# A residual block at its turn to gate_up: ScalarE's copies and halves of h2 in order, and the first y behind the third set's sums

## The chip, the cores and the metric

The kernel runs on one core of one Trainium2 chip. The metric is the device time of one execution in microseconds. Three executions before the change took 1344.05 us in the median (1343.78 to 1344.97).

## What is computed

One block of a hybrid encoder, for 1024 rows of 1024 numbers, all in float32:

```python
h = rmsnorm(x, norm_mix_pre)
m = mixer(h, ...)                 # gated short convolution + forgetting attention, merged, times w_out
x = x + rmsnorm(m, norm_mix_post)
h = rmsnorm(x, norm_ffn_pre)      # called h2 here
g, u = split(h @ w_gate_up)       # w_gate_up: 1024 x 5632, g and u 1024 x 2816
f = (silu(g) * u) @ w_down        # silu(g) = g * sigmoid(g)
x = x + rmsnorm(f, norm_ffn_post)
```

The change lies between the second `rmsnorm` and the first columns of `silu(g) * u`.

## The kernel before

Every float32 product is made of three matmuls of a rounded half and a rest: `split(hi, lo, src)` writes `hi` on ScalarE (a copy) and `lo = src - hi` on VectorE, and `mm3` multiplies hi·hi, hi·lo and lo·hi. The large products use a Strassen scheme with seven block products. For gate_up, the moving side is h2 in seven forms: B11, B21, B22 and the sums T1 to T4, each with a hi and a lo half. The stationary side is a pair of weight blocks for one column f of 128 (gate and up): A11, A12, A22 and the sums S1 to S4.

The tiles that matter here:

- `um`: h2, transposed, 8 x 128 x 1024. `e_norm(st)` (L1248) makes one slice of 128 rows: two sums of squares, a scale, the addition of x, a second scale into `tt`, the store of `xt` to `x2_dram`, eight TensorE transposes into `tp` and two ScalarE copies from `tp` into `um`. The eighth slice, st = 7, is the last.
- `hah`, `hal`: the halves of B11 and B21, from the first four slices.
- `hth`, `htl` and `hch`, `hcl`: the halves of T1 to T4 and of B22. `h2_sums(sl)` (L1317) makes them for one slice of each half of the rows, sl = 0 to 3, and needs slices sl and 4 + sl of `um`: on VectorE two sums into `sx` and two into tiles `c22`, on ScalarE the four hi halves, on VectorE the four lo halves.
- `raw` (3 buffers), `hi` (4), `lo` (3), `sx` (1), `s4` (1): the weights of a column as loaded, their halves and their sums.
- `c12`, `c21`, `c22` (2 buffers each): results of a column. In the profile they all appear as `c`, the PSUM banks as `b`.
- `z`: two buffers that xt, c11 (a column's first result, g1 below) and `sgf` (the sigmoid) take in turn.

The order of the stage as written: columns 0 to 6 (NPRE = 7) get their first two products early, since these need only B11 and B21. `f_first(f)` (L1282) makes A11·B11, copies it out (p1), goes on in the same bank with A12·B21, copies that out (c11, the first quarter of g) and stores both to `pre_dram`. `f_first(0)` to `f_first(3)` stand ahead of `e_norm(7)`, `f_first(4)` to `f_first(6)` between the four `h2_sums`. Then the loop over all 22 columns (L1361):

```python
for f in range(NF):
    if f < NPRE:
        p1 = t_(fp, "c21")
        nc.gpsimd.dma_start(p1, pre_dram[f][0])
        g1 = z_tile("c11", w=NC)
        nc.gpsimd.dma_start(g1, pre_dram[f][1])
        _, g2, u1_, u2 = strassen(rest.get(), hb, psm, fp, p1)
```

`strassen` (L505) makes the five products left, of 12 matmuls each, in the order S2·T2, S1·T1, S3·T3, S4·B22, A22·T4. Behind each stands a VectorE addition of the bank to a result; the first, `add(c12, p1, b2)`, reads p1 and has to be done before S3·T3 goes on in the same bank. c21 is the tile of p1. `rest.get()` keeps the operands of two columns ready: on its first call it prepares sets 0 and 1, on its second, in column 1, the third one, set 2. A set (`prep_rest`, L444) is two loads into `raw` and

```python
sub(s3, a11, a21)
add(s1, a21, a22)
sub(s2, s1, a11)
split(hx, lx, sx)      # S2 and S3
split(h2, l2, r2)      # S1 and A22
sub(s4, a12, s2)
split(h4, l4, s4)      # S4
```

After `strassen`, a column's y is made in `um` (free by then), half by half: a ScalarE sigmoid into `sgf`, `sgf * g` and `sgf * u` on VectorE. Every second column, `y_sums` makes sums of two y for the product with w_down and stores them to `a_dram` from GpSimd's queue.

What sets the order: Python only traces the instructions. A planner then writes out each engine's queue from its own reckoning of when operands and buffers are ready, so an instruction whose inputs are early may stand well ahead of its place in the source. At run time each engine works through its queue strictly in that order. Where `strict[0]` names an engine, each of its instructions is pinned behind the one traced last on that engine (L76: `keep_in_program_order`); the pin is an order, not a wait for the other to finish. In the stage of the change `strict[0]` was empty. All instructions pass through one helper, so the profile gives L74 as the line of all; tiles tell them apart.

Of the kernel before, what the change touches and what calls it, by code (L numbers as in the profile page):

```python
# [12 lines left out]
AF = mybir.ActivationFunctionType  # L13
# [8 lines left out]
ST = S // P  # L22
# [23 lines left out]
def block_kernel(  # L46
# [17 lines left out]
    strict = [()]  # L64

    class InOrder:
# [15 lines left out]
    nc = SimpleNamespace(  # L82
        **{e: InOrder(e) for e in engines}
    )
# [7 lines left out]
    def pool(name, bufs=1, side="left", space=None):  # L92
        kw = dict(name=name, bufs=bufs)
        if space is not DRAM:
            kw["reuse_waits"] = "tile"
        if space is not None:
            kw["space"] = space
        else:
            kw["side"] = side
        stack = ExitStack()  # L100
        ctx.callback(stack.close)
        return stack.enter_context(tc.tile_pool(**kw)), stack.close
# [4 lines left out]
    def add(o, a, b):  # L107
        nc.vector.tensor_tensor(o, a, b, op=ALU.add)
# [4 lines left out]
    def mul(o, a, b):  # L113
        nc.vector.tensor_tensor(o, a, b, op=ALU.mult)

    def copy(o, a):
        nc.scalar.activation(o, a, AF.Copy)
# [14 lines left out]
    cpool, _ = pool("const")  # L132
    stat, _ = pool("stat", 4, side="right")
    dpool, _ = pool("dram", space=DRAM)
# [40 lines left out]
    def st_tile(name, w=1):  # L175
        return stat.tile([P, w], F32, tag=name, name=name)
# [24 lines left out]
    def z_tile(name, dt=F32, w=S):  # L201
        return zp.tile([P, S], dt, tag="z", name=name, bufs=2)[:, :w]
# [146 lines left out]
    for st in range(ST):  # L349
        ops, rest = cur  # L350
# [19 lines left out]
    wpool, _ = pool("w")  # L370
# [107 lines left out]
    def bank(psp, name):  # L478
        return psp.tile([P, NC], F32, tag="mm", name=name)

    def prod(ps, w, b, first):
        (ah, al), (bh, bl) = w, b
        kw = {} if first else dict(skip_group_check=True)
        for k in range(4):
            mm3(
                ps,
                (ah[:, k, :], al[:, k, :]),
                (bh[:, k, :], bl[:, k, :]),
                first and k == 0,
                k == 3,  # L490
                **kw,
            )

    def t_(tmp, name):
        return tmp.tile([P, NC], F32, tag=name, name=name)
# [9 lines left out]
    def strassen(w, hb, psp, tmp, p1=None):  # L505

        b1 = None
        if p1 is None:
            b1 = bank(psp, "b1")
            prod(b1, w["A11"], hb[B11], True)  # L510
            p1 = t_(tmp, "c21")
            copy(p1, b1)
        b2, b3 = bank(psp, "b2"), bank(psp, "b3")
        prod(b2, w["S2"], hb[T2], True)
        c12 = t_(tmp, "c12")
        add(c12, p1, b2)
        prod(b3, w["S1"], hb[T1], True)
        c22 = t_(tmp, "c22")
        add(c22, p1, b3)
        if b1 is not None:  # L520
            prod(b1, w["A12"], hb[B21], False)
        prod(b2, w["S3"], hb[T3], False)
        add(c22, c22, b2)
        prod(b3, w["S4"], hb[B22], False)
        add(c12, c12, b3)
        prod(b2, w["A22"], hb[T4], False)
        c21 = p1
        add(c21, p1, b2)
        return b1, c12, c21, c22
# [21 lines left out]
    psm, psm_close = pool("psm", 6, space=PSUM)  # L551
    n1, n2 = slice(0, NC), slice(NC, S)

    def wcols(c0):
        return win[:, c0 : c0 + P]
# [270 lines left out]
    for ij, (kind, j, _, _) in enumerate(jobs):  # L826
# [4 lines left out]
        if ij < 2:  # L831
            if ij == 0:
# [7 lines left out]
                for n, (w, _) in enumerate(heads):  # L840
                    b1, b2 = bank(psm, "b1"), bank(psm, "b2")
                    p1, c11 = t_(pp, "c21"), t_(pp, "so")
# [14 lines left out]
            w = {**w, **(prep_rest(wcols(jobs[ij][3]), r1) if ij else rest0)}  # L857
            if ij == 1:
                pairs.q.append(pairs.prep(*pairs.srcs.popleft()))
            _, c12, c21, c22 = strassen(w, h1b, psm, pp, p1)  # L860
# [7 lines left out]
        else:  # L868
            w = pairs.get()
# [63 lines left out]
    def sg_tile():  # L933
        return tp_.tile([P, NC], F32, tag="sg", name="sg", bufs=4)
# [24 lines left out]
    was, sgs = {}, {}  # L959
# [203 lines left out]
    psm, psm_close = pool("psm2", 8, space=PSUM)  # L1163
# [30 lines left out]
    for n in range(2):  # L1194
        ns = slice(n * NC, (n + 1) * NC)
        for d in range(KT):
            ds_ = slice(d * P, (d + 1) * P)
            sg = sg_tile()
# [23 lines left out]
    fp, fp_close = pool("f", 2)  # L1222
# [20 lines left out]
    def load_xt(st):  # L1243
        xt = z_tile("xt")
        nc.sync.dma_start(xt, x2d[st * P : (st + 1) * P, :])
        return xt

    def e_norm(st, pm):  # L1248
        ss = slice(st * P, (st + 1) * P)
        xt = xts.popleft()  # L1250
        if st + 1 < ST:
            xts.append(load_xt(st + 1))
        tt = ep.tile([P, D], F32, tag="t", name="tt", bufs=1)
        s2 = st_tile("s2", 2)
        for n in range(2):
            ns = slice(n * NC, (n + 1) * NC)
            nc.scalar.activation(tt[:, ns], pm[n], AF.Square, accum_out=s2[:, n : n + 1])
        ssq = st_tile("ssq")
        add(ssq, s2[:, 0:1], s2[:, 1:2])
        rs = rms_scale(ssq)  # L1260
        for n in range(2):
            ns = slice(n * NC, (n + 1) * NC)
            nc.vector.scalar_tensor_tensor(
                tt[:, ns], pm[n], rs, gpo[:, ns], op0=ALU.mult, op1=ALU.mult
            )
        add(xt, xt, tt)
        nc.gpsimd.dma_start(x2_dram[ss, :], xt)
        ssq = st_tile("ssq")
        nc.scalar.activation(tt, xt, AF.Square, accum_out=ssq)
        rs = rms_scale(ssq)  # L1270
        nc.vector.scalar_tensor_tensor(tt, xt, rs, gpr, op0=ALU.mult, op1=ALU.mult)
        for q in range(2):
            tp = psm.tile([P, 4, P], F32, tag="mm", name="tp")
            for k in range(4):
                kt = 4 * q + k
                nc.tensor.transpose(tp[:, k, :], tt[:, kt * P : (kt + 1) * P], ident)
            copy(um[:, 4 * q : 4 * q + 4, ss], tp)

    def f_src(f):
        return wgu[:, f * P : (f + 1) * P], wgu[:, FH + f * P : FH + (f + 1) * P]  # L1280

    def f_first(f):  # L1282
        w, _ = prep_first(f_src(f)[0])
        b1, p1 = strassen_first(w, hb, psm, fp)
        c11 = t_(fp, "c12")
        copy(c11, b1)
        nc.gpsimd.dma_start(pre_dram[f][0], p1)
        nc.gpsimd.dma_start(pre_dram[f][1], c11)

    hb = [(hah[:, q], hal[:, q]) for q in range(2)]  # L1290
# [26 lines left out]
    def h2_sums(sl):  # L1317
        a = slice(sl * P, (sl + 1) * P)
        b = slice(NC + sl * P, NC + (sl + 1) * P)
        b11, b12 = um[:, 0:4, a], um[:, 0:4, b]  # L1320
        b21, b22 = um[:, 4:8, a], um[:, 4:8, b]
        u = wtile("sx", 1).rearrange("p (t k) s -> p t k s", t=2)
        sub(u[:, 0], b12, b11)
        sub(u[:, 1], b22, u[:, 0])
        split(hth[:, 0:2, :, a], htl[:, 0:2, :, a], u)
        for n, x in enumerate(((b22, b12), (b21, u[:, 1]))):
            w = t_(fp, "c22").rearrange("p (k s) -> p k s", k=4)
            sub(w, *x)
            split(hth[:, 2 + n, :, a], htl[:, 2 + n, :, a], w)
        split(hch[:, :, a], hcl[:, :, a], b22)  # L1330

    for sl in range(4):
        if 4 + sl < NPRE:
            f_first(4 + sl)
        h2_sums(sl)


    wd = wdn.rearrange("(k h p) d -> h p k d", h=2, p=P)
# [4 lines left out]
    def y_slot(f):  # L1343
        return um[:, 4 * (f // 2 % 2) + f % 2, :]
# [13 lines left out]

    rest = Pairs([f_src(f) for f in range(NPRE)], prep_rest_alone)
    whole = Pairs([f_src(f) for f in range(NPRE, NF)])  # L1360
    for f in range(NF):  # L1361
        if f < NPRE:
            p1 = t_(fp, "c21")
            nc.gpsimd.dma_start(p1, pre_dram[f][0])
            g1 = z_tile("c11", w=NC)
            nc.gpsimd.dma_start(g1, pre_dram[f][1])
            _, g2, u1_, u2 = strassen(rest.get(), hb, psm, fp, p1)
        else:
            g1, g2, u1_, u2 = strassen(whole.get(), hb, psm, fp)
        if f == NPRE - 1:  # L1370
            whole.q.append(whole.prep(*whole.srcs.popleft()))
        yf = y_slot(f)
        sgs = z_tile("sgf")
        for g, u, ns in ((g1, u1_, n1), (g2, u2, n2)):
            sg = sgs[:, ns]
            nc.scalar.activation(sg, g, AF.Sigmoid)
            mul(sg, sg, g)
            mul(yf[:, ns], sg, u)
        if f % 2:
            y_sums(f // 2)  # L1380
        if f == NF - 2:
            ra, rb = pairs_of(raw_t()), pairs_of(raw_t())
            nc.sync.dma_start(ra, a_dram["A11"][0].rearrange("k p c -> p k c"))
            nc.sync.dma_start(rb, wd[0][:, 0:2, n1])
            down0 = [(pairs_of(hi_t()), pairs_of(lo_t())) for _ in range(2)]
            split(*down0[0], ra)
            split(*down0[1], rb)
# [140 lines left out]
    p1, c22, c11, c12 = (quarter(s_) for s_ in (4, 6, 0, 2))  # L1528
# [109 lines left out]
```

## Time and profile before

| | |
|---|---|
| median of three runs | 1344.05 us (1343.78 to 1344.97) |
| the profiled execution's own time | 1344.87 us |
| its span, first to last instruction | 1343.1 us |
| granted TensorE clock, mean | 0.998 |
| stage of `f_first` and the h2 halves | from 701.5 us to 742.2 us |
| columns 0 to 6 | from 742.2 us to about 841 us |

The profile is one execution. PE is TensorE, DVE VectorE, ACT ScalarE, POOL GpSimd, SP the queue of most loads. A row of a timeline has the start, the duration, the engine, the operation, and output <- inputs by tile name; the bracket at its end says how long the engine had been idle before and what ended it. Matmuls overlap, so their starts, not their durations, tell the pace.

### The profile page before, as it was taken

The page shows a single profiled execution, that of the slowest core. Times are in us where ns is not written, and L with a number is a line of the kernel's source. Part 1 is how long each engine was busy: PE and PEld are TensorE (multiplying, and loading weights), DVE is VectorE, ACT ScalarE, POOL GpSimd, SP SyncE. Part 2 cuts the span into 40 slices and gives each one's busy share as a digit, 9 for nine tenths or more (in the row PEclk, how much of TensorE's full clock was granted, in tenths as well). Part 3 has the DMA queues.
Part 4 walks back from the last instruction along what each step waited for, and adds up shares of the span by engine and source line. Part 5 has one row for each costly group of instructions (what it writes and reads, how often), then busy time and mean ns, then how long its engine had stood idle before and what let it go on. Part 6 is the DMA issues. An engine that isn't in the chain of part 4 may idle for free. (4 is left out here: it accounts for less than half of the span.)

```text
span 1343.1 us, 17663 instructions
## 1 busy us (share of the span) xinstructions
PE 1320.6 (98%) x6725; PEld 1096.9 (82%) x6725; DVE 935.2 (70%) x1451; ACT 533.7 (40%) x851; POOL 127.2 (9%) x252
## 2 busy tenths in 40 slices
PE   7999999999999999999999999999999999999997
PEld 7988888888887878788887888888888888888886
DVE  6883767755546767775668898777677766677585
ACT  6641322243345756514446322223222323444452
POOL 0001000011112212000002121110011001000000
PEclk9999999999999999999999999999999999999999
DMA  7242422333325445362235554332333336966541
GB/s 221 91 122 87 136 61 79 119 123 97 108 89 173 158 142 189 105 218 79 94 124 174 185 186 155 103 116 71 112 106 114 101 104 244 366 233 197 157 165 63
DMA packets 153397, 186.86 MB, mean 139 GB/s; under 512 B 9424, under 2 KB 106768, under 8 KB 153312
## 3 DMA queue, kind: packets, MB, share of 16 engines
q1 hardware_dynamic: 138576, 137.19, 32.7%
q0 software_dynamic: 14736, 48.54, 9.5%
q8 instruction: 52, 0.85, 0.3%
q14 instruction: 33, 0.27, 0.1%
HBM read 136.62 MB, written 49.09 MB: 138 GB/s over the span
## 5 line engine op out<-in xcount | busy, mean ns | idle before, releaser
L74 DVE TENSOR_TENSOR c<-c,b 128x512 f32<-128x512 f32 x195 | 133.2, 683 | 85.5 <-PE b L74 67.1
L74 DVE TENSOR_TENSOR lo<-raw,hi 128x1024 fp32r<-128x1024 f32 (+1 forms) x93 | 112.1, 1205 | 82.5 <-PE b L74 70.5
L74 ACT ACTIVATE hi<-raw 128x1024 fp32r<-128x1024 f32 (+1 forms) x100 | 101.7, 1018 | 124.6 <-PE b L74 77.5
L74 PE MATMUL b<-hth,lo 128*128 128x512 f32 x352 | 137.1, 390 | 0.2 <-DVE lo L74 0.2
L74 PE MATMUL b<-hth,hi 128*128 128x512 f32 x352 | 137.1, 390 | 0.0
L74 ACT ACTIVATE hi<-sx 128x1024 fp32r<-128x1024 f32 x41 | 43.6, 1063 | 235.3 <-PE b L74 207.6
L74 PE MATMUL b<-htl,hi 128*128 128x512 f32 x352 | 137.0, 389 | 0.0
L74 PEld LDWEIGHTS b<-hth,lo 128*128 128x128 f32 x352 | 66.1, 188 | 14.3 <-DVE lo L74 0.6
L74 PEld LDWEIGHTS b<-hth,hi 128*128 128x128 f32 x352 | 66.1, 188 | 14.0 <-DVE c L74 0.3
L74 PEld LDWEIGHTS b<-htl,hi 128*128 128x128 f32 x352 | 66.1, 188 | 13.6
L74 DVE TENSOR_TENSOR lo<-sx,hi 128x1024 fp32r<-128x1024 f32 x41 | 50.2, 1224 | 31.1 <-PE b L74 29.4
L74 PE MATMUL b<-hah,hi 128*128 128x512 f32 x176 | 69.2, 396 | 1.8 <-ACT c L74 1.8
L74 PE MATMUL b<-hal,hi 128*128 128x512 f32 x176 | 69.3, 394 | 0.0
L74 PE MATMUL b<-hah,lo 128*128 128x512 f32 x176 | 69.0, 393 | 0.0
L74 DVE TENSOR_TENSOR sx<-raw 128x512 f32<-128x512 f32 x78 | 53.7, 688 | 20.6 <-DMA raw<-in_w_in_dram 10.6
L74 PE MATMUL pd<-hi,lo 128*128 128x512 f32 x160 | 62.3, 389 | 0.0
L74 PE MATMUL pd<-hi 128*128 128x512 f32 x160 | 62.0, 390 | 0.0
L74 PE MATMUL pd<-ghi 128*128 128x512 f32 x148 | 57.7, 390 | 0.0
L74 PE MATMUL pd<-glo,ghi 128*128 128x512 f32 x148 | 57.6, 389 | 0.0
L74 PE MATMUL pd<-ghi,glo 128*128 128x512 f32 x148 | 57.6, 389 | 0.0
L74 PE MATMUL b<-hT34h,hi 128*128 128x512 f32 x136 | 53.1, 390 | 0.4 <-DVE c L74 0.4
L74 PE MATMUL b<-hT12h,lo 128*128 128x512 f32 x136 | 52.9, 389 | 0.0
(362 smaller groups left out, 3361.7 us busy)
## 6 DMA issues: line engine op xcount, KB each, us to landing
raw<-in_w_gate_up_dram SPq DMA_DIRECT2D x51, 512.0 KB, 3.8
raw<-in_w_in_dram SPq DMA_DIRECT2D x35, 512.0 KB, 3.9
a_dramS<-um POOLq DMA_DIRECT2D x44, 256.0 KB, 2.8
a_dramA<-um POOLq DMA_DIRECT2D x33, 256.0 KB, 2.7
xt<-in_x_dram SPq DMA_DIRECT2D x16, 512.0 KB, 4.6
sg<-sg_dram SPq DMA_DIRECT2D x32, 256.0 KB, 4.3
graw<-a_dramS SPq DMA_DIRECT2D x14, 512.0 KB, 4.1
sg_dram<-c POOLq DMA_DIRECT2D x24, 256.0 KB, 2.3
```

The source lines that it names most:

```text
L74: ins = getattr(self.engine, name)(*args, **kw)
```

## The change

Three orders are pinned, and the first y is made later in the source. Nothing is computed otherwise.

- In `e_norm`, for st = 7, the two copies of `tp` into `um` are pinned on ScalarE.
- In `h2_sums(3)`, the four hi halves are pinned on ScalarE: each behind the one before, the first behind the last half of `h2_sums(2)`.
- The sigmoids and products of a column's y move into a function `silu_up`. For column 0 it is called in column 1, behind `rest.get()`, and both that call of `rest.get()` (set 2) and `silu_up(0)` are pinned on VectorE and ScalarE. The instruction traced ahead of set 2's first sum is column 0's last VectorE addition, `add(c21, p1, b2)`. For columns 0 to 6 `rest.get()` now stands ahead of the two loads from `pre_dram`.

```diff
+            if st == ST - 1:
+                strict[0] = ("scalar",)
             copy(um[:, 4 * q : 4 * q + 4, ss], tp)
+            strict[0] = ()
...
     for sl in range(4):
         if 4 + sl < NPRE:
             f_first(4 + sl)
+        if sl == 3:
+            strict[0] = ("scalar",)
         h2_sums(sl)
+    strict[0] = ()
...
+    def silu_up(f, blocks):
+
+        yf = y_slot(f)
+        sgs = z_tile("sgf")
+        for g, u, ns in blocks:
+            sg = sgs[:, ns]
+            nc.scalar.activation(sg, g, AF.Sigmoid)
+            mul(sg, sg, g)
+            mul(yf[:, ns], sg, u)
+
     for f in range(NF):
         if f < NPRE:
+            if f == 1:
+                strict[0] = ("vector", "scalar")
+            w = rest.get()
+            if f == 1:
+                silu_up(0, y0)
+                strict[0] = ()
             p1 = t_(fp, "c21")
             nc.gpsimd.dma_start(p1, pre_dram[f][0])
             g1 = z_tile("c11", w=NC)
             nc.gpsimd.dma_start(g1, pre_dram[f][1])
-            _, g2, u1_, u2 = strassen(rest.get(), hb, psm, fp, p1)
+            _, g2, u1_, u2 = strassen(w, hb, psm, fp, p1)
         else:
             g1, g2, u1_, u2 = strassen(whole.get(), hb, psm, fp)
         if f == NPRE - 1:
             whole.q.append(whole.prep(*whole.srcs.popleft()))
-        yf = y_slot(f)
-        sgs = z_tile("sgf")
-        for g, u, ns in ((g1, u1_, n1), (g2, u2, n2)):
-            sg = sgs[:, ns]
-            nc.scalar.activation(sg, g, AF.Sigmoid)
-            mul(sg, sg, g)
-            mul(yf[:, ns], sg, u)
+        blocks = ((g1, u1_, n1), (g2, u2, n2))
+        if f == 0:
+            y0 = blocks
+        else:
+            silu_up(f, blocks)
         if f % 2:
             y_sums(f // 2)
```

## The prediction

> **What bounds the kernel now.** I read the page's totals first, then TensorE's waits over the whole span, then the stage in which the one avoidable wait lies.
>
> ```profile
> span 1343.1 us, 17663 instructions
> PE 1320.6 (98%) x6725; PEld 1096.9 (82%) x6725; DVE 935.2 (70%) x1451; ACT 533.7 (40%) x851; POOL 127.2 (9%) x252
> ...
> PE tp L74 <- DVE hn L74: 7.8, 1, 7.8
> PE b L74 <- ACT c L74: 1.8, 1, 1.8
> ```
>
> TensorE is busy for 98% of the span, so an edit can only gain where TensorE stands still or runs slowly. Its longest wait is the start, 7.8 us. The next is one wait of 1.8 us for a ScalarE copy (ACT c), and it lies where the h2 halves are made. The windows around it (columns: window, its length, busy time and count of PE, PEld, DVE, ACT, POOL, granted clock, DMA share, GB/s) and the timelines of TensorE and ScalarE (start, duration, what; in brackets the idle time before and what ended it):
>
> ```profile
> 723.00:726.00 3.00, 1.17 (x6) 0.65 (x5) 0.69 (x1) 2.99 (x5) 0.31 (x1) 1.00 0.79 245
> 726.00:729.00 3.00, 3.00 (x10) 2.32 (x9) 1.90 (x3) 2.76 (x5) 0.77 (x2) 0.56 0.63 199
> ```
>
> ```profile
> 721.10 1.03 PE L74 MATMUL tp<-ident,tt 128*128 128x128 f32 x8
> ...
> 723.12 0.39 PE L74 MATMUL b<-hah,lo 128*128 128x512 f32 x1
> 725.34 0.50 PE L74 MATMUL b<-hah,hi 128*128 128x512 f32 x1 [1.83 <-ACT c L74]
> ...
> 726.81 0.63 PE L74 MATMUL b<-hah,lo 128*128 128x512 f32 x1
> 727.24 0.63 PE L74 MATMUL b<-hah,hi 128*128 128x512 f32 x1
> ...
> 729.79 0.40 PE L74 MATMUL b<-hah,hi 128*128 128x512 f32 x1
> ...
> 767.34 0.39 PE L74 MATMUL b<-hch,s4h 128*128 128x512 f32 x1
> ...
> 780.94 0.39 PE L74 MATMUL b<-hch,s4h 128*128 128x512 f32 x1
> ```
>
> ```profile
> 720.22 0.58 ACT L74 ACTIVATE c<-b 128x512 f32<-128x512 f32 x1
> 722.88 1.28 ACT L74 ACT_TABLE_LOAD   x1 [2.08 <-DMA x_dram<-xt]
> 724.17 0.63 ACT L74 ACTIVATE sgf<-c 128x512 f32<-128x512 f32 x1
> 724.71 0.58 ACT L74 ACTIVATE c<-b 128x512 f32<-128x512 f32 x1
> 725.18 1.08 ACT L74 ACTIVATE um<-tp 128x512 f32<-128x512 f32 x2
> ```
>
> The last view holds the story. At 720.80 ScalarE reaches the sigmoid of y 0, which the planner had floated up to this place. Its output tile sgf is one of two z buffers, and the store of xt has to leave it first: 2.08 us, then 1.28 us of table load, then the sigmoid. Queued behind it are the copy c, for which TensorE waits, and the copies of the last transposes into um, whose eight transposes began at 721.10. The copy starts at 724.71 and TensorE goes on at 725.34. Around 727 its matmuls start 0.43 us apart (726.81, 727.24), nearly twice the usual, and the granted clock of that stretch is 0.56.
>
> **The change, part by part.** *The early sigmoid goes (a gain).* y 0 is now traced behind the third set's sums, pinned there on ScalarE and VectorE, so no sigmoid can stand at 720.80. The copy c follows at once. From 723.12 to 729.79 there are 13 matmul starts in 6.67 us; at 0.227 us each (from column 1's fourth product at 767.34 to column 2's at 780.94 are 60 starts in 13.60 us) they take 2.95 us. The loss is **3.72 us**, 2.0 us of it standing still and 1.7 us at half rate. What is late next, if ScalarE is free? Nothing in this place: ScalarE stood idle there until the sigmoid's buffer was free.
>
> The Trainium skill, "TensorE: Matmul & The Clock Gate", section "Why this matters for your kernels", says that only a gap above about 3 us between bursts sends the clock back to half. The trace shows half rate after 1.83 us of idle time. By that rule the half-rate spell would have another cause than this gap and could stay (a rival below).
>
> *The halves of h2 (a small gain).* The pins hold the last slice's four halves on ScalarE in the order of the source. They can't start before um is copied, 725.18 before, about 722 after.
>
> ```profile
> 724.83 0.69 DVE L74 TENSOR_TENSOR sgf<-sgf,c 128x512 f32<-128x512 f32 x1 [1.85 <-ACT sgf L74]
> ...
> 741.72 1.23 DVE L74 TENSOR_TENSOR lo<-sx,hi 128x1024 fp32r<-128x1024 f32 x1 [0.40 <-ACT hi L74]
> ...
> 742.42 0.39 PE L74 MATMUL b<-htl,hi 128*128 128x512 f32 x1
> 743.00 0.50 PE L74 MATMUL b<-hth,lo 128*128 128x512 f32 x1 [0.18 <-DVE lo L74]
> ```
>
> Column 0's first product waits a little for set 0's low half: 743.00 less 742.42 less 0.23, or **0.35 us**. TensorE will arrive there 3.7 us earlier. VectorE's chain to that half starts with um, which comes about 3 us earlier, it stands still less between (1.85 us for the sigmoid), and it no longer makes the first product of y 0. I take the 0.35 us as gained; the bounds are that gain and a loss of 0.7 us (3.7 less 3).
>
> *The third set's sums and y 0 move back (a cost).* Set 2's first sum is now pinned on VectorE behind column 0's last addition, its halves follow in order, and y 0's sigmoids and products follow those. Times here are on the clock of before; all of it moves with TensorE.
>
> ```profile
> 752.39 0.69 DVE L74 TENSOR_TENSOR sx<-raw 128x512 f32<-128x512 f32 x1 [0.67 <-DMA raw<-in_w_gate_up_dram]
> ...
> 756.19 0.68 DVE L74 TENSOR_TENSOR s<-raw,sx 128x512 f32<-128x512 f32 x1
> ...
> 758.26 0.69 DVE L74 TENSOR_TENSOR sgf<-sgf,c 128x512 f32<-128x512 f32 x1
> 758.98 0.69 DVE L74 TENSOR_TENSOR um<-sgf,c 128x512 f32<-128x512 f32 x1
> 759.60 0.68 DVE L74 TENSOR_TENSOR c<-c,b 128x512 f32<-128x512 f32 x1
> ...
> 761.33 0.68 DVE L74 TENSOR_TENSOR um<-sgf,c 128x512 f32<-128x512 f32 x1
> ...
> 767.54 1.23 DVE L74 TENSOR_TENSOR lo<-raw,hi 128x1024 fp32r<-128x1024 f32 x1 [0.59 <-PE b L74]
> 768.68 0.68 DVE L74 TENSOR_TENSOR c<-c,b 128x512 f32<-128x512 f32 x1
> ```
>
> ```profile
> 756.99 0.63 ACT L74 ACTIVATE s4h<-s 128x512 fp32r<-128x512 f32 x1 [1.27 <-DVE s L74]
> 757.52 0.62 ACT L74 ACTIVATE sgf<-c 128x512 f32<-128x512 f32 x1
> ```
>
> The first sum goes from 752.39 to 760.28, behind the addition of 759.60. Set 2's second low half waited for a buffer until column 1's third product ended, 767.54, and still does. But S4's difference, 756.19 before, is traced behind it and is now pinned there: 768.68 to 769.37. Its high half follows 0.12 us later (756.87 to 756.99), at 769.49; the table load comes 0.53 us behind it (756.99 to 757.52), at 770.02; the sigmoid at 771.31 (722.88 to 724.17). The two products follow 0.66 and 0.72 us on (724.17 to VectorE's product at 724.83; 758.26 to 758.98), so the first half of y 0 is done at 773.38, where it was done at 762.01.
>
> Who waits for that? The buffer of c21, which that product reads, takes p1 of column 2, and column 2's first addition needs p1 ahead of its third product:
>
> ```profile
> 762.42 0.56 POOL L74 DMA_DIRECT2D a_dramA<-um  x1 [12.30 <-DVE um L74]
> 762.97 0.54 POOL L74 DMA_DIRECT2D c<-pre_dram  x1
> ...
> raw<-in_w_gate_up_dram SPq DMA_DIRECT2D x8, 512.0 KB, 4.3
> c<-pre_dram POOLq DMA_DIRECT2D x6, 256.0 KB, 3.4
> ```
>
> Behind the product come 0.41 us to GpSimd's store (762.01 to 762.42), 0.55 us to the load, 3.4 us to its landing: 777.74. The addition takes 0.68 us and hands over at about 778.5. TensorE wants that bank for its third product, 12 matmuls ahead of the fourth at 780.94, at 778.22. So the two meet, and I price a **stall of 0.3 us**; the ends are none (the load 0.3 us quicker) and 1.5 us (two additions of column 1, 0.6 us each, ahead of the products in VectorE's queue). S4's difference also stands ahead of the addition of 768.68, which then ends at 769.97, still before the product that wants its bank at 770.06 (767.34 and 12 matmuls): nothing.
>
> The loads on SP's queue move too: raw has three buffers, so set 3's second load waits for S4's difference and lands at 769.37 + 4.3 = 773.7. Four sums of 0.72 us and two halves of at most 1.23 us bring set 3's first operands to 779.0. Column 3 starts at 786.4 (780.94 less 36 matmuls of 0.227 us, plus 13.60), 7.4 us later. That lead is the cover; if VectorE fell 7.4 us behind, it would be gone. Eight VectorE operations (four sums, a low half, three products of y 0: those of 724.83, 758.26 and 758.98) move to the time behind 759.6, 5.5 us at 0.69 us, where VectorE (the third busy time) was nearly full:
>
> ```profile
> 759.20:772.80 13.60, 13.60 (x62) 11.26 (x61) 11.94 (x18) 4.03 (x6) 2.17 (x4) 1.00 0.62 183
> 772.80:786.40 13.60, 13.60 (x62) 11.27 (x61) 13.09 (x20) 3.98 (x6) 3.79 (x7) 1.00 0.59 196
> ```
>
> It had 2.2 us of 27.2 to spare there, so it falls about 3.3 us behind in these two columns, less than the lead of 7.4 us. I take nothing for it.
>
> GpSimd's queue: the load of p1 for column 1 is traced behind set 2 now, but SP and GpSimd carry no pin, and its own buffer, not its place, sets its time. The load of p1 for column 2 stands behind the store of y 0's first quarter, as before; it is counted above. Nothing is added to the work but the order: each sigmoid, product and table load is there once, before and after.
>
> *The sum.* -3.72 - 0.35 + 0.3 = **-3.8 us** on the profiled execution: its span of 1343.1 becomes 1339.3 us. That execution took 1344.87 us (1.77 us lie around the span), 0.8 us over the median of the runs, 1344.05; the same step from the median gives **1340.3 us**, 0.28% less. About 0.2%, or 2.7 us, is what a measurement of this kernel can tell from no change, so the forecast clears that by 1.1 us alone.
>
> **The rivals.** *The slow spell stays, or half the gain is eaten.* If the half-rate spell had another cause than the gap, only 2.0 + 0.35 us go and 0.3 come: 1342.0 us. (The Trainium skill's rule above would end here.) A stall of 1.5 us at column 2 in place of 0.3 ends close by, at 1341.5 us; so does the 0.7 us of loss at column 0, at 1341.4. For it speaks how close the two ends at 778.2 lie; against the first form, that the spell follows the longest gap of the stage at 1.1 us. Faster by less than 0.2%, so no change that shows. Chance 0.20.
>
> *VectorE's queue stands behind set 3's load: slower.* The planner writes each queue's order out ahead by its own reckoning, and it took the store of xt for earlier than it was: that is the 2.08 us of table load above. If it does so with set 3's second load, released at 769.37, set 3's four sums stand ahead of the first product of y 0. They start at 773.7 and end at 776.6; two products bring the first half to 778.0, and 0.41, 0.55, 3.4 and 0.8 us more bring column 2's first addition to 783.2, 5.0 us behind the 778.22 at which TensorE wants it. A gap of 1.83 us cost 1.7 us more at half rate, so this one costs 6.7 us or more: 1344.05 - 4.07 + 6.7 = 1346.7 us, slower by 0.2%, and more where the load lands late. It decides from a stall of 5 us; a shorter one leaves no change that shows. For it: TensorE has no other product to turn to there, since set 3 isn't ready either. Against it: y 0's products are traced ahead of set 3, and VectorE waited for such loads no more than 0.67 us (752.39). Chance 0.18.
>
> *The pins do nothing there.* If the sigmoid were merely moved to another early place, the time would stay. The pin on ScalarE runs from the sigmoid back through set 2's halves to the last addition of column 0, made at 759.60, so this is as good as excluded; it is in the 0.20.
>
> **How the numbers follow.** The forecast has 0.62: TensorE's gap and the spell go, and column 2 costs under 1 us. Its own range is 1339.9 (no stall) to 1341.3 us. The predicted time is its sum, 1340.3. The range must take in the second case, up to 1342.0 and its mixtures, and reaches to 1343.6; below it ends at 1339.7, where all of 4.07 us is gained and a little of what VectorE waits for. Left out are the slower case and some of the space between, 2 in 10. Faster by over 0.2% 0.62, within 0.2% 0.20, slower by over 0.2% 0.18.
>
> **What the profile of the changed kernel would show.** Right: no TensorE wait for ACT c near 723, no stretch with a granted clock under 1.00 there, the table load behind column 1's third product (about 766 on the new clock), and column 0's last addition (759.60 before) some 4 us earlier. The third step shows in TensorE's waits: at most one short wait for DVE c where column 2 has its third product, and a load c<-pre_dram that lands just ahead of it. Wrong: a wait there of 2 us or more, a second stretch below full clock, a wait of TensorE for lo of set 3, or VectorE waiting long for raw ahead of the products of y 0.

## The result and the profile after

The changed kernel takes **1347.42 us** in the median of 11 runs (1345.98 to 1348.87); the kernel before, run beside it, 1344.27 us (11 runs, 1343.50 to 1346.01). The ratio is 1.0021 [1.0012, 1.0029]: 3.2 us slower, where 3.8 us less was forecast. The forecast was 1340.3 us, with a range of 1339.7 to 1343.6 us. The profiled execution took 1348.38 us, its span 1346.6 us, against 1344.87 and 1343.1 before.

The page's first lines and two lines of TensorE's waits, of the changed kernel (the last three numbers: us in total, times, longest):

```profile
span 1346.6 us, 17666 instructions
PE 1321.8 (98%) x6725; PEld 1095.7 (81%) x6725; DVE 934.9 (69%) x1451; ACT 532.5 (40%) x851; POOL 127.2 (9%) x252
...
PE b L74 <- ACT hi L74: 3.0, 2, 2.7
PE b L74 <- DVE c L74: 1.1, 2, 0.7
```

The 1.8-us wait for ACT c is gone. In its place stand 2.7 us for a high half of weights and 0.7 us for an addition; the other 0.4 us for DVE c stood in before too. TensorE's timeline and the windows show where (same columns as in the prediction):

```profile
774.65 0.39 PE L74 MATMUL b<-hth,lo 128*128 128x512 f32 x1
777.78 0.50 PE L74 MATMUL b<-hth,hi 128*128 128x512 f32 x1 [2.74 <-ACT hi L74]
...
779.91 0.63 PE L74 MATMUL b<-hth,hi 128*128 128x512 f32 x1
780.34 0.63 PE L74 MATMUL b<-htl,hi 128*128 128x512 f32 x1
...
783.30 0.39 PE L74 MATMUL b<-hth,hi 128*128 128x512 f32 x1
...
788.54 0.39 PE L74 MATMUL b<-hch,s4l 128*128 128x512 f32 x1
789.64 0.50 PE L74 MATMUL b<-hth,hi 128*128 128x512 f32 x1 [0.71 <-DVE c L74]
```

```profile
774.00:777.00 3.00, 1.04 (x5) 0.54 (x3) 3.00 (x6) 0.33 (x1) 2.21 (x5) 1.00 0.57 197
777.00:780.00 3.00, 1.92 (x6) 0.98 (x7) 3.00 (x5) 2.71 (x4) 1.52 (x3) 0.97 0.83 255
780.00:783.00 3.00, 3.00 (x9) 2.32 (x8) 2.49 (x5) 0.00 (x0) 0.64 (x2) 0.50 0.80 249
```

Column 2 begins at 769.44, 24 matmuls ahead of the gap; before it began at 772.78. So 3.34 us had been gained up to there. From 774.65 to 783.30 there are 14 steps in 8.65 us, which at 0.227 us take 3.18: 5.47 us lost, some 3 of it standing still and the rest at half rate. The step from 788.54 to 789.64 loses 0.87. That is 6.3 us back, a net loss of 3.0; the spans differ by 3.5, and the last half microsecond is lost further on.

VectorE's own timeline tells why it came to this (same kernel):

```profile
750.43 1.22 DVE L74 TENSOR_TENSOR lo<-raw,hi 128x1024 fp32r<-128x1024 f32 x1 [2.03 <-PE b L74]
...
753.15 0.69 DVE L74 TENSOR_TENSOR c<-c,b 128x512 f32<-128x512 f32 x1 [0.90 <-PE b L74]
755.87 0.69 DVE L74 TENSOR_TENSOR c<-c,b 128x512 f32<-128x512 f32 x1 [2.03 <-PE b L74]
756.48 0.69 DVE L74 TENSOR_TENSOR sx<-raw 128x512 f32<-128x512 f32 x1
...
768.63 0.69 DVE L74 TENSOR_TENSOR sgf<-sgf,c 128x512 f32<-128x512 f32 x1 [0.65 <-ACT sgf L74]
769.24 0.68 DVE L74 TENSOR_TENSOR sx<-raw 128x512 f32<-128x512 f32 x1
...
775.87 0.68 DVE L74 TENSOR_TENSOR sx<-raw 128x512 f32<-128x512 f32 x1
...
780.61 1.28 DVE L74 TENSOR_TENSOR c<-c,b 128x512 f32<-128x512 f32 x2
```

Set 2's first sum (756.48) stands right behind column 0's last addition (755.87), as the pin says. In the three waits ahead of it VectorE stood idle for 4.96 us; in its pinned order nothing could come earlier, though set 2's load need not have been missing (in a run below without this pin it had landed by 749.76). The debt falls due from 768.63 on: no bracket follows until 780.61, so VectorE works without a pause through the products of y 0 and y 1, their four sums, and set 3. Column 2's first two additions (780.61, x2) come 11.2 us behind the column's start. Before, the first came 4.35 us behind it:

```profile
777.13 0.68 DVE L74 TENSOR_TENSOR c<-c,b 128x512 f32<-128x512 f32 x1
```

In TensorE's queue the planner put 13 matmuls of column 3 ahead of column 2's third product, and those need set 3's halves. These are late for the same reason: the sum at 775.87 is followed by ScalarE's high half, which ends at 777.73, and TensorE goes on at 777.78. ScalarE's own timeline:

```profile
758.73 1.06 ACT L74 ACTIVATE hi<-sx 128x1024 fp32r<-128x1024 f32 x1 [11.96 <-DVE sx L74]
...
772.79 1.16 ACT L74 ACTIVATE sgf<-c 128x512 f32<-128x512 f32 x2 [3.67 <-DMA c<-pre_dram]
776.67 1.06 ACT L74 ACTIVATE hi<-sx 128x1024 fp32r<-128x1024 f32 x1 [2.73 <-DVE sx L74]
```

Two more things stand in it. Set 2's halves are pinned on ScalarE too, but ScalarE had waited 11.96 us for VectorE's sum (758.73), so it was VectorE's order that held set 2 back; no run takes the pin off one of the two engines alone. And the late y 0 makes y 1 late: y 0's first product frees the buffer into which column 1's c11 is loaded, that load is issued at 769.73, and y 1's sigmoids (772.79) wait for it. So the products of both fall into VectorE's full stretch.

### The profile page after: what moved, and what is told of

It reads as the page before. It is cut to its first block, busy times and chain, and to the rows that moved or that the text cites. A ratio compares the mean times of both kernels' runs of the same rounds, so it can differ in the third digit from the quotient of the medians.

```text
span 1346.6 us, 17666 instructions
## 1 busy us (share of the span) xinstructions
PE 1321.8 (98%) x6725; PEld 1095.7 (81%) x6725; DVE 934.9 (69%) x1451; ACT 532.5 (40%) x851; POOL 127.2 (9%) x252
## 4 chain that ended last, share of the span: by engine, by line
PE 60%; DVE 2%; ACT 1%; DMA 1%; issue 0%; DVEq 0%; ACTq 0%
PE b L74 30%; PE pd L74 16%; PE pm L74 5%; PE pbb L74 3%; PE pba L74 2%; PE po L74 1%; PE tps L74 1%; PE sp L74 1%; DMA raw<-in_w_gate_up_dram 1%; DVE um L74 0%; PE tp L74 0%; ACT tt L74 0%; DVE tt L74 0%; DVE lo L74 0%; DVE hal L74 0%
## 5 line engine op out<-in xcount | busy, mean ns | idle before, releaser
L74 PE MATMUL b<-hT34h,lo 128*128 128x512 f32 x136 | 52.9, 389 | 0.0
```

The costliest lines, as they stand in the source:

```text
L74: ins = getattr(self.engine, name)(*args, **kw)
```

## The experiments

The theories, by the letters of the expectations: **A**, VectorE's queue is late, because the pin puts set 2 (and with it y 0, pinned behind it) behind column 0's last addition; **B**, the buffer of p1 for column 2 comes free too late, since y 0's product reads it late (the prediction's own chain); **D**, the order that the planner wrote for TensorE's queue (column 3's matmuls early) makes the wait. Diffs are against the changed kernel, except where they say otherwise.

**One part alone.** First the change without its pins on the h2 copies and halves (only y 0 and set 2 move):

```diff
-            if st == ST - 1:
-                strict[0] = ("scalar",)
...
-        if sl == 3:
-            strict[0] = ("scalar",)
```

> Only the other half of the change: y 0 behind set 2, both pinned on VectorE and ScalarE; no pins on the copies into um and the h2 halves. A and B: everything the change does comes from this half: early stall gone, late stall there, 1347 us as the change. If the h2 pins carry a part of the gain or the loss: 1 us or more away from the change.

Measured: 1347.14 us (9 runs), ratio 1.0027 [1.0017, 1.0037]. TensorE's queue has the order of the full change, and the same wait:

```profile
777.50 0.50 PE L74 MATMUL b<-hth,hi 128*128 128x512 f32 x1 [2.73 <-ACT hi L74]
```

Then the kernel before with only those pins on the h2 copies and halves:

```diff
-            if f == 1:
-                silu_up(0, y0)
...
+            _, g2, u1_, u2 = strassen(rest.get(), hb, psm, fp, p1)
```

> Only the first two pins of the change: the last copies into um and the last slice's halves on ScalarE; y 0 untouched. A and B: the sigmoid floats up as before, the stall at 723 and the half rate stay, 1343.8 to 1344.5 us. The rival reading of the change's first half (these pins remove the stall): about 1340.5 us.

Measured: 1345.64 us (10 runs), ratio 1.0014 [1.0005, 1.0023]. The sigmoid stays where it was, and so does the early gap, at 725.14. Its windows:

```profile
725.14 0.50 PE L74 MATMUL b<-hah,hi 128*128 128x512 f32 x1 [1.58 <-ACT c L74]
...
756.76 0.50 PE L74 MATMUL b<-hth,hi 128*128 128x512 f32 x1 [1.03 <-DVE c L74]
```

```profile
726.00:729.00 3.00, 3.00 (x15) 2.48 (x14) 2.71 (x4) 3.00 (x7) 0.57 (x2) 1.00 0.56 185
```

So the wait at column 2 belongs to the part with y 0 and set 2. The pins on ScalarE alone bring nothing. In this profile TensorE waits 1.5 us for additions of column 0 (the row of 756.76 and one of 0.50 us), behind a wait of 1.71 us of VectorE for set 2's load; that this is the pins' doing is not shown, since the kernel before has such a wait in one of its two profiles (the last run below). And here a 1.58-us gap is followed by a full clock, 1.00: the half rate of the prediction does not follow every such gap.

**The buffer of p1.** Column 0's c21 goes to a free piece of `um`, so that p1's buffer doesn't wait for y 0:

```diff
-        c21 = p1
+        c21 = p1 if c21 is None else c21
...
+            away = um[:, 6, n1] if f == 0 else None
+            _, g2, u1_, u2 = strassen(w, hb, psm, fp, p1, away)
```

> The change, but column 0's c21 is written to a free piece of um, so that the buffer of p1 is free for column 2's load with column 0's last addition, and not with y 0. B: the load lands early and the late stall goes, 1340.5 to 1341.5 us. A: column 2's first addition stands where it stood in VectorE's full queue, and the stall stays: 1347 us.

Measured: 1346.86 us (10 runs), ratio 1.0023 [1.0014, 1.0032].

```profile
777.25 0.50 PE L74 MATMUL b<-hth,hi 128*128 128x512 f32 x1 [2.73 <-ACT hi L74]
```

The wait is the same to 0.01 us. B falls. In the changed kernel the load of p1 for column 2 was issued at 771.48, and with the 3.4 us that such loads take it was there near 774.9, 5.7 us ahead of the addition that reads it. In this run it was issued at 756.45, 15 us earlier, and the wait stayed. The row of the changed kernel, then that of this run:

```profile
771.48 0.54 POOL L74 DMA_DIRECT2D c<-pre_dram  x1
...
756.45 0.54 POOL L74 DMA_DIRECT2D c<-pre_dram  x1 [10.69 <-DVE um L74]
```

**VectorE relieved.** The four sums of y 0 and y 1 (`y_sums(0)`), about 0.6 us each in VectorE's queue, are left out of the work; their stores stay.

```diff
+        if k:
+            add(ops["S1"], y1[:, n2], ops["A22"])
...
```

> The change, with the four VectorE sums of the first pair of y (S1 to S4 for the product with w_down) left out; they stand in VectorE's queue ahead of column 2's first addition and take 4 x 0.61 us. A: that addition and set 3's halves come 2.4 us earlier, so the stall of about 3 us shrinks to 1 us or less and the half-rate spell with it: 1341.5 to 1344 us. B: y 0 comes no earlier, so 1347 us.

Measured: 1343.61 us (10 runs), ratio 1.0000 [0.9991, 1.0009].

```profile
775.35 0.50 PE L74 MATMUL b<-hth,hi 128*128 128x512 f32 x1 [0.21 <-ACT hi L74]
776.78 0.50 PE L74 MATMUL b<-hth,lo 128*128 128x512 f32 x1 [0.69 <-DVE lo L74]
784.82 0.50 PE L74 MATMUL b<-hth,hi 128*128 128x512 f32 x1 [0.94 <-DVE c L74]
```

With 2.4 us less in VectorE's queue, the 2.74 us shrink to 0.21, and the time is 3.25 us less than that of the run before on the same chip (1346.86 us), which had the full wait. That is more than was taken away: no half-rate spell follows the short waits (the granted clock is 1.00 from 774 to 786). This speaks for A.

**TensorE in the source's order.** The change, and TensorE pinned to the order of the source in columns 2 and 3:

```diff
+            if f in (2, 3):
+                strict[0] = ("tensor",)
             _, g2, u1_, u2 = strassen(w, hb, psm, fp, p1)
+            strict[0] = ()
```

> The change, with TensorE's matmuls of columns 2 and 3 pinned in the order of the source, so that no product of column 3 stands ahead of column 2's third. Theory D (the order of TensorE's queue is the loss: column 3's products are waited for while column 2's could run): about 1341 to 1342 us. A: column 2's third product has to wait for its first addition, which stands in VectorE's queue at 780.6 against 774.9 when TensorE is there: a stall of some 6 us and the half-rate spell behind it, 1347.5 to 1349 us, no better than the change.

Measured: 1350.66 us (5 runs), ratio 1.0050 [1.0037, 1.0062].

```profile
774.24 0.39 PE L74 MATMUL b<-hth,lo 128*128 128x512 f32 x1
780.94 0.79 PE L74 MATMUL b<-hth,hi 128*128 128x512 f32 x1 [6.31 <-DVE c L74]
...
786.23 0.63 PE L74 MATMUL b<-hch,s4h 128*128 128x512 f32 x1
```

D falls: the reordering was a relief, not the cause. Without it TensorE waits for column 2's first addition itself, 6.31 us, as A has it, and then runs 0.43 us a step to 786.65.

**Set 2 free, y 0's sigmoids pinned.** y 0 returns to its own column, and only its sigmoids are pinned on ScalarE, so that they can't float up to 720; the pins on h2 stay.

```diff
-            if f == 1:
-                strict[0] = ("vector", "scalar")
...
+            strict[0] = ("scalar",)
+        silu_up(f, blocks)
+        strict[0] = ()
```

> y 0 is made in its own column again, with its sigmoids alone pinned on ScalarE (behind set 1's last half); set 2 carries no pin; the pins of the h2 halves stay. Theory A (set 2's pin wastes VectorE's time ahead of column 0's last addition, and column 2's first addition then stands too late in a full queue): no stall at column 2, the early stall gone, 1344.3 - 3.9 = about 1340.4 us. Theory B (y 0 late, so the buffer of column 2's p1 late): also 1340.4, y 0 being early. Theory C (the early stall's 3.7 us can't be had, since TensorE then only arrives earlier at operands that aren't there): 1343.5 to 1344.5.

Measured: 1342.84 us (11 runs), ratio 0.9992 [0.9984, 1.0001], between the two numbers expected. No wait is left at column 2, as A and B both say. But new ones stand in column 0. TensorE and VectorE:

```profile
751.19 0.47 PE L74 MATMUL b<-hch,s4h 128*128 128x512 f32 x1 [1.43 <-DVE c L74]
754.77 0.50 PE L74 MATMUL b<-hth,hi 128*128 128x512 f32 x1 [0.59 <-DVE c L74]
```

```profile
749.76 0.69 DVE L74 TENSOR_TENSOR sx<-raw 128x512 f32<-128x512 f32 x1 [2.94 <-DMA raw<-in_w_gate_up_dram]
750.37 0.68 DVE L74 TENSOR_TENSOR c<-c,b 128x512 f32<-128x512 f32 x1
```

Set 2's first sum waits 2.94 us for its load (0.67 and 1.97 us in the two profiles of before), and column 0's second addition, for which TensorE waits, is queued behind it. That is what becomes late next once TensorE reaches column 0 3.6 us earlier.

**The same with set 2's pin put back.**

```diff
-                strict[0] = ("vector", "scalar")
             w = rest.get()
...
+            strict[0] = ()
```

(That is the run above and, for `rest.get()` in column 1, `strict[0] = ("vector", "scalar")`.)

> As the one before, but set 2's sums and halves pinned on VectorE and ScalarE as in the change; y 0 stays in its own column. A: a stall at columns 2 and 3 like that of the change, somewhat shorter because y 0's products use VectorE's free time: 1344 to 1347 us. B: y 0 is early, so p1 is early and no stall comes: 1340.4 us.

Measured: 1344.46 us (11 runs), ratio 1.0004 [0.9996, 1.0013].

```profile
775.08 0.50 PE L74 MATMUL b<-hth,hi 128*128 128x512 f32 x1 [0.37 <-ACT hi L74]
776.02 0.50 PE L74 MATMUL b<-hth,hi 128*128 128x512 f32 x1 [0.21 <-ACT hi L74]
784.03 0.50 PE L74 MATMUL b<-hth,hi 128*128 128x512 f32 x1 [1.14 <-DVE c L74]
```

```profile
776.20 0.68 DVE L74 TENSOR_TENSOR c<-c,b 128x512 f32<-128x512 f32 x1
```

The waits at column 2 return with set 2's pin alone, smaller than in the change, since here VectorE made products of y 0 in part of its idle time. On the same chip this cost 1.6 us against the run above. Column 2's first addition (776.20) comes 7.1 us behind the column's start at 769.11, against 4.35 before and 11.2 in the change. So set 2's pin alone makes 2.7 of the 6.8 us by which that addition slips; the rest comes with y 0 behind it, and with it the step from 1344.46 us to the 1347 us of the change.

**y 0 late, set 2 free.** The change, but the pin begins behind `rest.get()`:

```diff
             if f == 1:
-                strict[0] = ("vector", "scalar")
             w = rest.get()
             if f == 1:
+                strict[0] = ("vector", "scalar")
                 silu_up(0, y0)
```

> The change with set 2's sums free again and only y 0 pinned behind them on VectorE and ScalarE. A: VectorE makes the sums in its free time, y 0 follows, no stall: 1340 to 1341.5 us. B: y 0's place in the source is as late as in the change, but it is pinned to things that end early, so nearly the same; B allows 1340.4 to 1342.

Measured: 1342.70 us (11 runs), ratio 0.9990 [0.9981, 0.9999]. Nothing waits at column 2; in column 0 TensorE waits 0.71 and 0.73 us for additions, and VectorE 2.14 us for set 2's load. But y 0 is late here in the source alone. Set 2's sums begin at 749.52, and y 0's first product on VectorE follows at 756.38, where it came at 768.63 in the change:

```profile
756.38 0.69 DVE L74 TENSOR_TENSOR sgf<-sgf,c 128x512 f32<-128x512 f32 x1 [0.59 <-ACT sgf L74]
```

So y 0's place behind set 2 does no harm as long as set 2 is early. In the change set 2's pin holds back both, and the run above shows that either part has its price. No run makes y 0 as late as in the change with set 2 early.

**Set 2 in the middle of column 0.** The last three runs. Set 2 is prepared inside column 0's products, and only its first sum is pinned, behind column 0's third addition; y 0 stands in its own column with pinned sigmoids, and the pins on h2 stay. The pin keeps that sum from standing ahead of an addition while its load is under way, and gives VectorE set 2 to work on before column 0 ends.

```diff
     def prep_rest(src2, r1, pin=False):
...
+        if pin:
+            strict[0] = ("vector",)
         sub(s3, a11, a21)
+        strict[0] = () if pin else strict[0]
...
+            if f == 0:
+                mid = lambda: rest.q.append(rest.prep(*rest.srcs.popleft(), True))
+            _, g2, u1_, u2 = strassen(w, hb, psm, fp, p1, mid)
```

> The halves of h2 stay pinned. y 0 stays in its own column with its two sigmoids pinned on ScalarE. Set 2 is prepared in the middle of column 0's products, and of it only the first sum is pinned on VectorE, behind column 0's third addition (that of S3*T3). Theory A (VectorE's queue is what was late: full after 768 in the change because set 2's sums came at 756) expects no wait at column 2: set 2's sums start about 752, and VectorE has no 5 us of idle time ahead of them. The load theory (without the pin, set 2's first sum waits 2 to 3 us for its load ahead of column 0's second addition, and TensorE waits 1.4 to 2 us for that) expects no wait of VectorE for raw ahead of column 0's first three additions, and none of TensorE there above 0.3 us. Both together: 1340.5 to 1341.5 us, about 2.5 us under before. If the waits in column 0 come from VectorE's other work (the low halves of set 1) and not from the load, they stay: about 1342.7 us as without the pin. If VectorE is late at column 2 all the same, 1344 us or more.

Measured: **1341.10 us** (9 runs, 1340.74 to 1341.35) against 1344.55 us of before in the same set (19 runs), ratio 0.9975 [0.9965, 0.9985]. It is faster than before, and than the changed kernel, which ran in another set. Its waits have one line left of the kind, the 0.4 us that stood in before too, and VectorE's timeline shows set 2 at 751.91 with no wait for its load, and column 2's first addition 5.0 us behind that column's start (769.01):

```profile
PE b L74 <- DVE c L74: 0.4, 1, 0.4
```

```profile
751.31 0.68 DVE L74 TENSOR_TENSOR c<-c,b 128x512 f32<-128x512 f32 x1
751.91 0.68 DVE L74 TENSOR_TENSOR sx<-raw 128x512 f32<-128x512 f32 x1
...
774.02 0.68 DVE L74 TENSOR_TENSOR c<-c,b 128x512 f32<-128x512 f32 x1
```

The same one product earlier, behind the second addition:

```diff
+        if mid:
+            mid()                      # behind the addition of S1*T1
...
-        if mid:
-            mid()                      # behind the addition of S3*T3
```

> As the run with the pin behind column 0's third addition, but one product earlier, behind its second addition (that of S1*T1). The load theory expects this place to be too early for one thing: set 2's sums then stand ahead of the third addition in VectorE's queue, so the second addition no longer waits for the load, but the third may, by what is left of the load's time (up to 1 us): 1341 to 1342.5 us. Theory A expects no wait at column 2 here either. If the two places give the same time within 0.5 us, the place within column 0 does not matter, only that the load's wait is off the second addition.

Measured: 1342.02 us (11 runs), ratio 0.9984 [0.9975, 0.9993]. VectorE meets the load there, as expected, and TensorE waits 0.33 us for the third addition, which is queued behind set 2's sums:

```profile
748.34 0.69 DVE L74 TENSOR_TENSOR sx<-raw 128x512 f32<-128x512 f32 x1 [0.50 <-DMA raw<-in_w_gate_up_dram]
```

**The kernel before once more.**

> The kernel before, unchanged, for one more profile. If the half-rate spell behind the 1.8-us wait for ACT c comes only in some executions, this one may show the wait (1.6 to 1.9 us) without the spell, a granted clock of 1.00 behind it, and a time of 1343 to 1343.5 us; with the spell 1344.5 us or more. If the spell belonged to the wait in every execution, the profile would show it again.

Measured: 1346.06 us in one execution, with the gap and the spell:

```profile
725.13 0.50 PE L74 MATMUL b<-hah,hi 128*128 128x512 f32 x1 [1.99 <-ACT c L74]
...
726.38 0.63 PE L74 MATMUL b<-hal,hi 128*128 128x512 f32 x1
726.81 0.63 PE L74 MATMUL b<-hah,lo 128*128 128x512 f32 x1
```

```profile
726.00:729.00 3.00, 3.00 (x9) 2.32 (x8) 1.90 (x3) 2.55 (x5) 0.56 (x2) 0.50 0.57 184
```

It also has a wait in column 0 that the first profile of this kernel lacks, behind set 2's load:

```profile
753.49 0.69 DVE L74 TENSOR_TENSOR sx<-raw 128x512 f32<-128x512 f32 x1 [1.97 <-DMA raw<-in_w_gate_up_dram]
```

```profile
757.42 0.50 PE L74 MATMUL b<-hth,hi 128*128 128x512 f32 x1 [1.19 <-DVE c L74]
```

## Why the prediction was wrong

- **The early gap: right in kind, the size that of one execution.** Wait and spell are gone after the change, and column 2 began 3.34 us earlier. But the 1.7 us at half rate were taken as a part of every execution. The profile with the 1.58-us gap has a full clock behind it, so the step from one profiled execution to the median overstated the term for executions without the spell; there only about 2 us were to be had. The executions of before spread by over 3 us (1343.05 to 1346.19 in the last set). The mean granted clock recorded for each goes with this: over the three sets of the experiments, 47 of 77 executions had 0.999 and took 1343.4 to 1343.8 us in the mean of a set, eight had 0.997 and took 1345.8 to 1346.0. So slow matmuls come and go between executions, though the record does not say where in the span. The wait for set 2's load comes and goes too (0.67 and 1.97 us).
- **The halves of h2: the gain came, not by the pins.** The 0.35 us at column 0's first product are gone in the change, but also in the run without the pins on h2; with those pins alone a wait of 0.21 us for a high half stands there.
- **Column 2's third product: the right place, the wrong chain.** The load of p1 came when it was forecast (774.9; the forecast was 777.74 less the 3.34 us that TensorE was early, so 774.4), and so did y 0's first half (done at 770.5; forecast 773.38 less 3.34, so 770.0). The load was not what decided: taken off the path, it changed nothing.
- **The step that failed: "it falls about 3.3 us behind in these two columns, less than the lead of 7.4 us. I take nothing for it."** The backlog was measured against the start of column 3, as if set 3's operands were the only thing it delayed. Column 2's own additions stand in the same queue, and their lead is far shorter: before, the first was issued at 777.13 and done at 777.81, 0.4 us ahead of the 778.22 at which TensorE wanted its bank. A backlog of 3.3 us could not hide there. It was also too small: VectorE stood idle for 5 us at 748 to 756, and its first addition came 11.2 us into column 2 where it had come 4.35, a slip of 6.8 us, of which 2.7 are set 2's pin alone and the rest y 0 behind it (with y 1, which y 0 delays).
- **The slower rival: its price, by luck, and not its cause.** It gave 1346.7 us by a wait of 5 us at this very product, with set 3 ahead of y 0 in VectorE's queue; measured was 1347.42 us. But y 0's first product (768.63) stood ahead of set 3's first sum (769.24), which had no load to wait for; the way by p1 is refuted; and so is what the rival said for itself: the planner did turn TensorE to column 3, whose operands were not ready, and this cut a wait of 6.31 us to 2.74. What it said against itself, that VectorE waited for such loads no more than 0.67 us, held for one execution only.
- **What is late next, asked once too few.** The prediction asked it for the early gap and found nothing "in this place". In column 0 there was something: with set 2 free, its load is awaited in VectorE's queue ahead of an addition (2.94 us). The change's pin did remove this wait, at a higher price later. With both avoided the time is 1341.10 us, 3.45 us under before in its set; the forecast's sum was 3.8. Against the nine executions of before in that set with a clock of 0.999 (1343.71 us in the mean) it is 2.6 us, close to the 2.35 us that the forecast has without the spell.

## What to carry to other kernels

When work is moved later on an engine that executes in order, compare the backlog with the shortest lead of anything queued on that engine, not with the lead of the operands that were moved: here additions with 0.4 us to spare stood behind sums with 7.4. A pin that keeps work behind an engine's idle time costs it that idle time, and here the cost showed where the engine was next full, two columns on; what is pinned behind the late work adds to it. Time gained ahead of a load turns into a wait for that load unless the load's first reader stands behind the work that others wait for.

## What the runs showed of the chip

The length of a gap and the clock behind it, over seven profiles: 1.58 us of idle time, full rate (1.00); 1.83 us, half rate (0.56 in a 3-us window); 1.99 us, 0.50; 2.74 us, 0.50; 2.73 us in two more runs, 0.60 and 0.57; 6.31 us, half rate for the longest stretch, from 780.94 to 786.65. So a gap of 1.83 us in this kernel cost nearly as much again in slow matmuls, one of 1.58 us did not; whether length alone decides, seven gaps can't tell. The spell need not begin with the first matmul behind the gap: in the changed kernel TensorE goes on at 777.78 and the steps become 0.43 us only from 779.91. The Trainium skill, "TensorE: Matmul & The Clock Gate", section "Why this matters for your kernels", puts the length that resets the clock at about 3 us; here half rate followed gaps of 1.83 and 1.99 us, and the measurement decides.
